# Hybrid encoder trunk: the last output projection computed as two Strassen products

## The chip, the cores and the metric

The kernel runs on one NeuronCore of a Trainium2 chip. The metric is the device time of one execution in microseconds; the figure for the kernel before is the median of three runs. The profile is of one separate execution.

## What is computed

Two encoder layers over 512 tokens with 2048 features, then an RMS norm, all in float32. Cut to what matters:

```python
def hybrid_layer(x, ...):
    proj = rms_norm(x, norm_w) @ w_in                  # 2048 -> 6144 columns
    o_attn = attention(q, k, v)                        # 1024 features
    o_conv = c_b * conv3(c_c * c_in)                   # 512
    o_sgu  = gelu(u) * (W_s norm(gelu(v)) + b)         # 512
    mixed  = concat(rms_norm(o_i, branch_w_i) * silu(gate_i))   # 2048
    return x + mixed @ w_out                           # 2048 -> 2048
y = rms_norm(layer2(layer1(x)), final_norm_w)
```

## The kernel before

Feature tiles (128 features on the partitions, 512 tokens along them) are kept as pairs: `split` writes a rounded part H on ACT (L96) and the rest L on DVE (L97). `product` takes one block of 512 output columns: `load_pair` (L76) fetches the weights of two feature tiles in one 512 KB transfer into a `wr` buffer, each tile is split into `wH` and `wL` (`split_weight`, L183 and L184, where a column scale is needed), and for each of the four output tiles three matmuls (L202) are added up: H·H, L·H, H·L. A product is 16 tiles x 4 x 3 = 192 matmuls. The pool `wp` gives `wr`, `wH` and `wL` three buffers each, so weights can be split at most a little ahead of the matmuls. The output projection reads the feature tiles `mH[0..15]`, `mL[0..15]`: tiles 0 to 7 are attention (`mA`), 8 to 11 convolution (`mc`), 12 to 15 the gating unit (`ms`).

The gating unit is last. After the last input projection (`win[l, 11]`) its rows go through Silu (L495), a multiply (L496), a block transpose on DVE (`tr.put`, L143), a 1 MB write to DRAM (`mv<-blk`, L149), four reads back (`rearr<-mv`, L153) and the split into `ms` tiles.

In layer 2 the output projection gives token-major rows. Blocks 0 to 2 of 512 columns are `product` calls; the residual x of each is rebuilt by `residual(b)`: an add of xH and xL (L527), a DVE transpose (L529), a write `mx<-p` (L531) and reads `xt<-mx` (L534). Row sums of squares are collected on ACT (L550), and the rows are multiplied by the final norm weight on GpSimd (L551). Block 3 is done last from weights that are all split ahead into `wfH`, `wfL` (in the freed `x{k}` buffers), one tile of 128 tokens after another, so that the end of each tile (L599 to L613) runs under the matmuls of the next.

The order of the instructions on each engine's queue is not that of the program: it is planned when the kernel is built (`TileContext(nc, schedule_with_timeline_sim=True)`), with an estimated duration for each instruction. Of the instructions whose inputs and buffers are free by that plan, the one that is earlier in the program goes first. On the chip each queue keeps that order. All large transfers are issued by SyncE (SP).

Of the kernel before, what the change touches and what calls it, by code (L numbers as in the profile page):

```python
# [8 lines left out]
F32 = mybir.dt.float32  # L9
# [5 lines left out]
P = 128  # L15
# [6 lines left out]
NQ = 8  # L22
NKV = 2
EPS = 1e-6
SCALE = HD ** -0.5


def f32(ap):
    return ap.bitcast(F32)
# [3 lines left out]
def trunk_kernel(ctx: ExitStack, tc: tile.TileContext, xT, win, wout, wcols, convw, qkw, sgun,  # L33
# [15 lines left out]
    def nm(s):  # L49
        uid[0] += 1  # L50
        return f"{s}_{uid[0]}"
# [134 lines left out]
    def product(src, cols, Hs, Ls, feature_major, before=None):  # L186
# [16 lines left out]
                                         stop=(k == KT - 1 and i == 2))  # L203
        return acc

    sqx = Squares()

    xraw = [big.tile([P, 4, S], F32, tag="mA", name=f"xraw{i}", bufs=4) for i in range(4)]
# [12 lines left out]
    def load_both(kp):  # L221
# [14 lines left out]
            first.append(broadcast_x(first[0]))  # L236
        return raw

    for l in range(L):
        banks.update(seq=["acc"] * 4, at=0)  # L240
        wc = lay.tile([P, 2, KT], F32, tag="wc", name=nm("wc"), bufs=2)
        nc.scalar.dma_start(out=wc, in_=wcols[l])
# [157 lines left out]

        mH, mL = [None] * KT, [None] * KT

        def finish(sq, inv, os, first, dst):
            R = broadcast_rows(token_rstd(sq.t, inv, "b"))
            for i, o in enumerate(os):
                nc.vector.scalar_tensor_tensor(out=o, in0=o, scalar=wc[:, 1, first + i:first + i + 1], in1=R,
                                               op0=ALU.mult, op1=ALU.mult)
                h_, l_ = dst(i)
                split(h_, l_, o)
                mH[first + i], mL[first + i] = h_, l_  # L410

        sqc = Squares()
# [33 lines left out]
        mA = [big.tile([P, ST, S], F32R, tag="mA", name=nm("mA"), bufs=4) for _ in range(4)]  # L446
        finish(sqa, 1.0 / 1024, oat, 0, lambda i: (mA[i // 4][:, i % 4], mA[2 + i // 4][:, i % 4]))

        finish(sqc, 1.0 / 512, oc, 8,
               lambda i: tuple(big.tile([P, S], F32R, tag="qb", name=nm("mc"), bufs=8) for _ in range(2)))  # L450

        acc = product(win[l, 9], nw, xH, xL, False)
        vnH = big.tile([P, ST, S], F32R, tag="kv", name=nm("vnH"), bufs=2)
# [45 lines left out]
        for st in range(ST):  # L499
            tr.put(st, gu[:, st])  # L500
        tr.move()
        for e in range(4):
            mH[12 + e], mL[12 + e] = [big.tile([P, S], F32R, tag="qa", name=nm("ms"), bufs=8) for _ in range(2)]
            split(by_block(mH[12 + e]), by_block(mL[12 + e]), tr.get(e))

        if l < L - 1:
            sqx = Squares()
            for b in range(4):
                acc = product(wout[l, b], bw, mH, mL, True)
                for e in range(4):  # L510
                    d = 4 * b + e
                    t = T()
                    nc.vector.tensor_tensor(out=t, in0=acc[e], in1=f32(xL[d]), op=ALU.add)
                    nc.vector.tensor_tensor(out=t, in0=t, in1=f32(xH[d]), op=ALU.add)
                    sqx.add(t)
                    split(xH[d], xL[d], t)

    fr = [lay.tile([P, S], F32, tag=tag, name=nm("fr")) for tag in ("sn", "swH", "swL", "Rx")]
    for b in range(4):
        nc.sync.dma_start(out=fr[b], in_=frow[b * S:(b + 1) * S].partition_broadcast(P))  # L520
    def residual(b):
        e_ = big.tile([P, 4, 4, P], F32, tag="o" if b == 0 else "kv", name=nm("xt"), bufs=1 if b == 0 else 2)
        m = dram.tile([P, 4, 4, P], F32, tag="mx", name=nm("mx"))
        for e in range(4):
            d = 4 * b + e
            t = T()
            nc.vector.tensor_tensor(out=t, in0=f32(xH[d]), in1=f32(xL[d]), op=ALU.add)  # L527
            blk = T("p")
            nc.vector.transpose(out=blk.rearrange("p (b s i) -> p s b i", b=4, i=32),  # L529
                                in_=t.rearrange("p (s b j) -> p s b j", b=4, j=32))  # L530
            nc.sync.dma_start(out=m[:, e], in_=blk.rearrange("p (b f) -> p b f", b=4))  # L531
        mv = m.rearrange("(a j) e b f -> b j e a f", a=4)
        for q in range(4):
            nc.sync.dma_start(out=e_[32 * q:32 * q + 32], in_=mv[q])  # L534
        return e_.rearrange("p e a (s i) -> p s (e a) i", i=32)
# [5 lines left out]
    xt = []  # L541
    for b in range(3):
        xt.append(residual(b))
        acc = product(wout[L - 1, b], bw, mH, mL, False)
        for st in range(ST):
            v = xt[b][:, st]
            nc.vector.tensor_tensor(out=v, in0=grouped(acc[st]), in1=v, op=ALU.add)
        for st in range(ST):
            v = xt[b][:, st]
            nc.scalar.activation(grouped(T()), v, AF.Square, accum_out=sums[st][:, b:b + 1])  # L550
            nc.gpsimd.tensor_tensor(out=v, in0=v, in1=grouped(fr[b]), op=ALU.mult)  # L551

    xq = [T("qr") for _ in range(ST)]
    m = dram.tile([P, 4, 4, P], F32, tag="mx", name=nm("mx"))
    for e in range(4):
        t = T()
        nc.vector.tensor_tensor(out=t, in0=f32(xH[12 + e]), in1=f32(xL[12 + e]), op=ALU.add)
        blk = T("p")
        nc.vector.transpose(out=blk.rearrange("p (b s i) -> p s b i", b=4, i=32),
                            in_=t.rearrange("p (s b j) -> p s b j", b=4, j=32))  # L560
        nc.sync.dma_start(out=m[:, e], in_=blk.rearrange("p (b f) -> p b f", b=4))
        nc.gpsimd.tensor_copy(out=xq[3][:, e * P:(e + 1) * P], in_=t[:, 3 * P:])
    mv = m.rearrange("(a j) e b (s i) -> b s j e a i", a=4, i=32)
    for st in range(3):
        for q in range(4):
            nc.sync.dma_start(out=xq[st][32 * q:32 * q + 32].rearrange("p (e a i) -> p e a i", e=4, a=4),
                              in_=mv[q, st])

    wf = []
    for kp in range(KT // 2):  # L570
        raw = load_pair(wout[L - 1, 3, kp])
        for j in range(2):
            k = 2 * kp + j
            H = res.tile([P, S], F32R, tag=f"x{k}", name=f"wfH{k}", bufs=2)
            Lo = res.tile([P, S], F32R, tag=f"x{k}", name=f"wfL{k}", bufs=2)
            split_weight(raw[:, j], bw(k), H, Lo)
            wf.append((H, Lo))
    part = sm.tile([P, ST], F32, tag="part", name="part", bufs=1)
    accs = accumulators()
    for st in range(ST):  # L580
        ss = slice(st * P, (st + 1) * P)
        p_ = part[:, st:st + 1]
        nc.vector.tensor_reduce(out=p_, in_=sums[st][:, :3], axis=AX.X, op=ALU.add)
        nc.vector.tensor_scalar(out=p_, in0=p_, scalar1=1.0 / D, scalar2=EPS, op0=ALU.mult, op1=ALU.add)
        acc = accs[st]
        if st == 3:
            for e in range(4):
                es = slice(e * P, (e + 1) * P)
                nc.tensor.matmul(acc[:, es], xq[3][:, es], ident, start=(e == 0), stop=False)
        for k in range(KT):  # L590
            H, Lo = wf[k]
            nc.tensor.matmul(acc, mH[k][:, ss], H, start=(st < 3 and k == 0), stop=False)  # L592
            nc.tensor.matmul(acc, mL[k][:, ss], H, start=False, stop=False)  # L593
            nc.tensor.matmul(acc, mH[k][:, ss], Lo, start=False, stop=(k == KT - 1))  # L594
        su = small(1)
        y = acc
        if st < 3:
            y = xq[st]
            nc.vector.tensor_tensor(out=y, in0=acc, in1=y, op=ALU.add)  # L599
        nc.scalar.activation(T(), y, AF.Square, accum_out=su)  # L600
        v = small(1)
        nc.vector.tensor_scalar(out=v, in0=su, scalar1=1.0 / D, scalar2=p_, op0=ALU.mult, op1=ALU.add)
        r = small(1)
        nc.gpsimd.tensor_tensor(out=r, in0=v, in1=negh[:, :1], op=ALU.pow)
        for b in (0, 2, 1, 3):
            o = T("p" if b % 2 else "t")
            if b == 3:
                nc.vector.scalar_tensor_tensor(out=o, in0=y, scalar=r, in1=fr[3], op0=ALU.mult, op1=ALU.mult)
            elif b == 2:
                nc.vector.tensor_scalar(out=grouped(o), in0=xt[b][:, st], scalar1=r, scalar2=None, op0=ALU.mult)  # L610
            else:
                nc.scalar.activation(grouped(o), xt[b][:, st], AF.Copy, scale=r)
            nc.sync.dma_start(out=out[ss, b * S:(b + 1) * S], in_=o)  # L613


def _columns():
# [51 lines left out]
```

## Time and profile before

| | |
|---|---|
| median of 3 runs | 1524.43 us (1522.11 to 1527.09) |
| span of the profiled execution | 1521.4 us, first to last instruction |
| TensorE busy | 1503.8 us (99%), 6630 matmuls |
| VectorE, ScalarE, GpSimd busy | 887.7, 625.5 and 74.5 us |
| DMA | 203.09 MB, mean 133 GB/s |

The page gives no other time of the profiled execution than its span; the span is 3.0 us under the median of the runs. The span runs from the first to the last instruction, and busy shares are means over stages with different limits.

### The profile page before, as it was taken

The page shows a single profiled execution, that of the slowest core. Times are in us where ns is not written, and L with a number is a line of the kernel's source. Part 1 is how long each engine was busy: PE and PEld are TensorE (multiplying, and loading weights), DVE is VectorE, ACT ScalarE, POOL GpSimd, SP SyncE. Part 2 cuts the span into 40 slices and gives each one's busy share as a digit, 9 for nine tenths or more (in the row PEclk, how much of TensorE's full clock was granted, in tenths as well). Part 3 has the DMA queues.
Part 4 walks back from the last instruction along what each step waited for, and adds up shares of the span by engine and source line. Part 5 has one row for each costly group of instructions (what it writes and reads, how often), then busy time and mean ns, then how long its engine had stood idle before and what let it go on. Part 6 is the DMA issues. An engine that isn't in the chain of part 4 may idle for free.

```text
span 1521.4 us, 18115 instructions
## 1 busy us (share of the span) xinstructions
PE 1503.8 (99%) x6630; PEld 1240.6 (82%) x6630; DVE 887.7 (58%) x1652; ACT 625.5 (41%) x1057; POOL 74.5 (5%) x72
## 2 busy tenths in 40 slices
PE   9999999999999999999999999999999999999997
PEld 7888878888888888888888887888888888878876
DVE  7667788745446534454446777896454573445562
ACT  7334365544334433333334344564343443332342
POOL 0111000000000100000000110000000010001120
PEclk9999999999999999999999999999999999999999
DMA  7345566733323334333334346676333333465544
GB/s 265 111 103 148 175 194 202 204 100 98 97 87 96 102 96 139 111 97 87 108 93 124 110 134 183 208 207 180 97 97 97 91 97 104 139 168 152 136 160 139
DMA packets 75402, 203.09 MB, mean 133 GB/s; under 512 B 14256, under 2 KB 21680, under 8 KB 72496
## 3 DMA queue, kind: packets, MB, share of 16 engines
q1 hardware_dynamic: 75024, 201.90, 45.4%
q8 instruction: 52, 0.85, 0.2%
q14 instruction: 38, 0.31, 0.1%
q10 hardware_dynamic: 288, 0.03, 0.0%
HBM read 169.39 MB, written 32.51 MB: 133 GB/s over the span
## 4 chain that ended last, share of the span: by engine, by line
PE 91%; DMA 4%; DVE 2%; issue 1%; ACT 1%; SPq 0%; ACTq 0%; POOLq 0%; DVEq 0%
PE acc L202 64%; PE sc L202 19%; DMA rearr<-mv 1%; DMA mv<-blk 1%; PE ps L371 1%; PE ps L372 1%; PE ps L370 1%; PE sc L344 1%; PE sc L345 1%; PE sc L346 1%; DMA wr<-in_wout 1%; PE sc L594 1%; DMA xt<-mx 0%; PE sc L592 0%; PE sc L593 0%
## 5 line engine op out<-in xcount | busy, mean ns | idle before, releaser
L184 DVE SCALAR_TENSOR_TENSOR wL<-wr,wc,wH 128x512 fp32r<-128x512 f32 x412 | 306.0, 747 | 395.8 <-ACT wH L183 376.9
L183 ACT ACTIVATE wH<-wr,wc 128x512 fp32r<-128x512 f32 x412 | 296.3, 723 | 532.2 <-PE acc L202 418.8
L202 PE MATMUL acc<-xL,wH 128*128 128x512 f32 x672 | 261.4, 389 | 0.0
L202 PE MATMUL acc<-xH,wH 128*128 128x512 f32 x672 | 260.8, 389 | 0.0
L202 PE MATMUL acc<-xH,wL 128*128 128x512 f32 x672 | 245.2, 389 | 0.0
L202 PE MATMUL acc<-wH,xH 128*128 128x512 f32 x608 | 237.2, 391 | 0.7 <-ACT wH L183 0.6
L202 PE MATMUL acc<-wH,xL 128*128 128x512 f32 x608 | 236.8, 390 | 0.0
L202 PE MATMUL acc<-wL,xH 128*128 128x512 f32 x608 | 213.5, 390 | 0.1
L202 PEld LDWEIGHTS acc<-xH,wH 128*128 128x128 f32 x672 | 126.2, 188 | 26.4
L202 PEld LDWEIGHTS acc<-xL,wH 128*128 128x128 f32 x672 | 126.1, 188 | 26.3
L202 PEld LDWEIGHTS acc<-xH,wL 128*128 128x128 f32 x672 | 126.1, 188 | 26.1
L202 PEld LDWEIGHTS acc<-wH,xH 128*128 128x128 f32 x608 | 114.2, 188 | 26.0 <-ACT wH L183 1.8
L202 PEld LDWEIGHTS acc<-wL,xH 128*128 128x128 f32 x608 | 113.9, 188 | 24.3 <-DVE wL L184 0.5
L202 PEld LDWEIGHTS acc<-wH,xL 128*128 128x128 f32 x608 | 114.3, 188 | 23.7
L97 DVE TENSOR_TENSOR wL<-wr,wH 128x512 fp32r<-128x512 f32 x84 | 57.4, 691 | 96.9 <-ACT wH L96 77.4
L96 ACT CAST wH<-wr 128x512 fp32r<-128x512 f32 x84 | 52.1, 623 | 134.3 <-PE acc L202 80.8
L353 ACT ACTIVATE p<-sc,sa 128x512 f32<-128x512 f32 x64 | 43.8, 685 | 62.2 <-DVE sa L350 58.0
L202 PE MATMUL sc<-wH,xL 128*128 128x512 f32 x160 | 62.3, 389 | 0.0
L202 PE MATMUL sc<-wH,xH 128*128 128x512 f32 x160 | 62.3, 389 | 0.0
L103 POOL TENSOR_TENSOR s<-s,negh 128x4 f32<-128x4 f32 (+2 forms) x40 | 43.3, 1082 | 371.4 <-DVE s L101 358.7
L202 PE MATMUL sc<-wL,xH 128*128 128x512 f32 x160 | 59.7, 390 | 0.0
L114 POOL TENSOR_TENSOR rc<-s,negh 128x4 f32<-128x4 f32 x6 | 7.6, 1273 | 881.3 <-DVE s L113 881.3
(259 smaller groups left out, 2214.5 us busy)
## 6 DMA issues: line engine op xcount, KB each, us to landing
wr<-in_win SPq DMA_DIRECT2D x191, 512.0 KB, 3.7
wr<-in_wout SPq DMA_DIRECT2D x64, 512.0 KB, 3.7
mv<-blk SPq DMA_DIRECT2D x22, 1024.0 KB, 4.7
rearr<-mv SPq DMA_DIRECT2D x88, 256.0 KB, 5.3
mx<-p SPq DMA_DIRECT2D x16, 256.0 KB, 3.1
xraw<-in_xT SPq DMA_DIRECT2D x7, 512.0 KB, 9.8
xt<-mx SPq DMA_DIRECT2D x12, 256.0 KB, 5.8
out_y<-t SPq DMA_DIRECT2D x8, 256.0 KB, 2.7
```

What stands on the lines that cost most here:

```text
L96: nc.scalar.copy(H, src)
L97: nc.vector.tensor_tensor(out=Lo, in0=src, in1=f32(H), op=ALU.subtract)
L103: nc.gpsimd.tensor_tensor(out=r, in0=v, in1=negh[:, :n], op=ALU.pow)
L183: nc.scalar.activation(wH, raw, AF.Copy, scale=c)
L184: nc.vector.scalar_tensor_tensor(out=wL, in0=raw, scalar=c, in1=f32(wH), op0=ALU.mult, op1=ALU.subtract)
L202: nc.tensor.matmul(acc[e], a, b, start=(k == 0 and i == 0), stop=(k == KT - 1 and i == 2))
L344: nc.tensor.matmul(sc, qH[:, ss], kH, start=True, stop=False)
L345: nc.tensor.matmul(sc, qH[:, ss], kL, start=False, stop=False)
L346: nc.tensor.matmul(sc, qL[:, ss], kH, start=False, stop=True)
L353: nc.scalar.activation(p, sc, AF.Exp, scale=SCALE, bias=nm_, accum_out=su)
L370: nc.tensor.matmul(po, a, pH[:, t], start=(t == 0), stop=False)
L371: nc.tensor.matmul(po, a, pL[:, t], start=False, stop=False)
```

## The change

The 2048 x 2048 output projection of layer 2 is taken as two products, each over two column blocks (0 and 1, then 2 and 3). In each, the contraction is cut into features 0 to 1023 and 1024 to 2047, the tokens into two halves of 256, and the columns into the two blocks. Seven half products (p = 1 to 7; each 8 feature tiles x 2 token tiles x 3 matmuls) stand for eight. What is needed for that:

- Sums and differences of the feature tiles (`differences`, four DVE operations on 128 x 256 for each k of 0 to 7), then split (`sums_of`) into the `x{k}` buffers. For k = 0 to 3 they are made after `finish`, before `win[l, 9]`; for k = 4 to 7 they need the gating unit's tiles, which are first scaled and copied on ACT (`raw`).
- Sums of weights, made by transfers: GpSimd issues transfers that add DRAM rows to a loaded buffer (`add_rows`, with `accum_op`). X[kp] is loaded for p = 1 and added to for p = 5, 6 and 4; p = 7 loads a `wr` buffer and adds to it.
- Three pairs of accumulator banks: p = 1, 6, 7, 4 use `c1`, p = 5, 3 use `c2`, p = 2 uses `c3`; the rows xt are added to or subtracted from after each.
- The residual's transposes and writes to DRAM move into layer 1's output projection, 16 of each; the adds xH + xL are gone. In layer 2 only the reads are left.
- At the end p = 4 of the second product is held: weights split ahead, 24 matmuls for each token tile. `leave(st)` takes the place of L596 to L613; the identity matmuls are gone.

```diff
+        if last:
+            for k in range(4):
+                v = nraw[k // 2][:, k % 2]
+                differences(v[:, 0], v[:, 1], v[:, 2], v[:, 3], oat[k], oc[k])
...
+        if last:
+            for k in range(4):
+                sums_of(k, v[:, 0:2], v[:, 2:4])
         for e in range(4):
-            split(by_block(mH[12 + e]), by_block(mL[12 + e]), tr.get(e))
+            nc.scalar.activation(by_block(raw), tr.get(e), AF.Copy, scale=wc[:, 1, 12 + e:13 + e])
+            split(mH[12 + e], mL[12 + e], raw)
+            differences(n12[:, 0], n12[:, 1], n34[:, 0], n34[:, 1], oat[4 + e], raw)
+            sums_of(4 + e, n12, n34)
...
+                    nc.vector.transpose(out=blk.rearrange("p (b s i) -> p s b i", b=4, i=32),
+                                        in_=t.rearrange("p (s b j) -> p s b j", b=4, j=32))
+                    nc.sync.dma_start(out=rowsd[b][:, e], in_=blk.rearrange("p (b f) -> p b f", b=4))
...
+    def add_rows(dst, src):
+        nc.gpsimd.dma_start(out=dst, in_=src, accum_op=ALU.add)
...
+        def weights(p, kp):
+            if p == 1:
+                nc.sync.dma_start(out=X[kp], in_=s0[kp])
+                return X[kp]
+            if p == 2:
+                return load_pair(s0[4 + kp])
+            if p == 3:
+                return load_pair(s1[4 + kp])
+            if p == 7:
+                y = load_pair(s1[4 + kp])
+                add_rows(y, s1[kp])
+                return y
+            add_rows(X[kp], {5: s1[kp], 6: s1[4 + kp], 4: s0[4 + kp]}[p])
+            return X[kp]
...
+        for p in order:
+            for kp in range(4):
+                w = weights(p, kp)
+                for j in range(2):
+                    split(H, Lo, w[:, j])
+                    for t in range(2):
+                        matmuls(bank[t], p, k, t, H, Lo)
...
+    pair(0, 1, (1, 2, 5, 6, 3, 7, 4), False)
+    residual(2)
+    residual(3)
+    pair(2, 3, (1, 5, 6, 3, 7, 2, 4), True)
```

## Rows read from the trace of the kernel before

**Rows 1.** The page: busy time of each engine, share, instructions.

```profile
PE 1503.8 (99%) x6630; PEld 1240.6 (82%) x6630; DVE 887.7 (58%) x1652; ACT 625.5 (41%) x1057; POOL 74.5 (5%) x72
```

**Rows 2.** The chain in order of time, layer 1: start us, us, what.

```profile
671.59 43.52 PE acc L202 x192
```

**Rows 3.** Timeline of PE: start us, us, engine, line, operation.

```profile
1334.73 0.61 PE L202 MATMUL sc<-wH,mA 128*128 128x512 f32 x2
...
1360.29 0.73 PE L202 MATMUL sc<-wH,mc 128*128 128x512 f32 x2 [0.92 <-ACT wH L96]
...
1513.10 0.39 PE L594 MATMUL acc<-wfL,ms 128*128 128x512 f32 x1
```

**Rows 4.** Windows: length; PE, PEld, DVE, ACT, POOL busy (count); clock; DMA share; GB/s.

```profile
1356.50:1367.40 10.90, 9.91 (x43) 7.57 (x42) 5.50 (x9) 5.20 (x9) 0.00 (x0) 1.00 0.62 168
...
1470.00:1482.00 12.00, 10.74 (x47) 8.41 (x46) 12.00 (x22) 5.57 (x12) 7.93 (x8) 1.00 0.28 95
```

**Rows 5.** Groups by line: count, busy us, mean ns, idle before.

```profile
L97 DVE TENSOR_TENSOR wL<-wr,wH 128x512 fp32r<-128x512 f32 x84 | 57.4, 691 | 96.9 <-ACT wH L96 77.4
...
L96 ACT CAST wH<-wr 128x512 fp32r<-128x512 f32 x84 | 52.1, 623 | 134.3 <-PE acc L202 80.8
...
L302 DVE TENSOR_TENSOR t<-t,cs 128x256 f32<-128x256 f32 x32 | 12.0, 416 | 0.1
...
L551 POOL TENSOR_TENSOR xt<-xt,fr 128x512 f32<-128x512 f32 x12 | 18.7, 1585 | 153.4 <-ACT t L550 153.4
...
L103 POOL TENSOR_TENSOR s<-s,negh 128x1 f32<-128x1 f32 x8 | 5.0, 626 | 85.2 <-DVE s L101 84.9
```

**Rows 6.** Groups by line, DVE, 1400 to 1440 us.

```profile
L527 DVE TENSOR_TENSOR t<-xH,xL 128x512 f32<-128x512 f32 x4 | 5.8, 1492 | 0.0
```

**Rows 7.** Timeline of SP and ACT, the gating unit's way in layer 2.

```profile
1340.48 0.33 SPq L149 DMA_DIRECT2D mv<-blk  x1
...
1340.86 3.69 SPq L534 DMA_DIRECT2D xt<-mx  x4
...
1346.12 2.71 SPq L153 DMA_DIRECT2D rearr<-mv  x4
...
1359.09 0.62 ACT L96 CAST ms<-rearr 128x512 fp32r<-128x512 f32 x1 [5.96 <-DMA rearr<-mv]
```

**Rows 8.** Timeline of SP and ACT, the same way in layer 1.

```profile
590.14 0.33 SPq L149 DMA_DIRECT2D mv<-blk  x1
...
603.43 1.14 ACT L96 CAST ms<-rearr 128x512 fp32r<-128x512 f32 x2 [4.85 <-DMA rearr<-mv]
```

**Rows 9.** Window after the last matmul, columns as in rows 4.

```profile
1518.00:1521.40 3.40, 0.00 (x0) 0.00 (x0) 0.00 (x0) 0.00 (x0) 0.00 (x0) 0.60 0.43 150
```

**Rows 10.** Timeline of PE, the first matmuls.

```profile
1.44 4.63 PE L89 MATMUL pw<-onesr 128*128 128x512 f32 x10 [1.44 <-DVE onesr L84]
```

**Rows 11.** The page: DMA issues, KB each, median us to landing.

```profile
wr<-in_wout SPq DMA_DIRECT2D x64, 512.0 KB, 3.7
...
mv<-blk SPq DMA_DIRECT2D x22, 1024.0 KB, 4.7
```

**Rows 12.** Tile view of rearr, 1340 to 1400 us.

```profile
DMA to landing us min/median/max: 9.3/10.3/10.8
```

**Rows 13.** Windows at the ends of layer 1's output blocks.

```profile
716.00:727.00 11.00, 11.00 (x51) 9.09 (x50) 10.62 (x18) 6.30 (x12) 0.00 (x0) 1.00 0.32 93
...
760.00:765.00 5.00, 4.93 (x22) 3.77 (x22) 4.84 (x9) 2.09 (x5) 0.00 (x0) 1.00 0.05 19
```

**Rows 14.** Timeline of the end: ACT and SP.

```profile
1513.57 0.60 ACT L600 ACTIVATE t<-acc 128x512 f32<-128x512 f32 x1 [8.10 <-issue]
...
1516.65 0.90 SPq L613 DMA_DIRECT2D out_y<-p  x2
```

**Rows 15.** Windows before and during that way.

```profile
1330.00:1340.00 10.00, 10.00 (x46) 8.29 (x45) 6.59 (x11) 5.48 (x8) 0.00 (x0) 1.00 0.30 95
...
1340.00:1360.00 20.00, 19.37 (x86) 15.71 (x84) 4.65 (x8) 4.02 (x7) 0.00 (x0) 1.00 0.99 236
```

More of the change, by code (lines that the diff above doesn't have):

```diff
@@ L24 @@
 EPS = 1e-6
+HALF = S // 2
 SCALE = HD ** -0.5
@@ L204, in product, with differences, sums_of @@
         return acc
+    NT = [None] * 8
+    def differences(n1, n2, n3, n4, lo, hi):
+        a, b = lo[:, :HALF], lo[:, HALF:]
+        c, d = hi[:, :HALF], hi[:, HALF:]
+        nc.vector.tensor_tensor(out=n1, in0=b, in1=d, op=ALU.subtract)
+        nc.vector.tensor_tensor(out=n2, in0=n1, in1=a, op=ALU.subtract)
+        nc.vector.tensor_tensor(out=n3, in0=a, in1=b, op=ALU.subtract)
+        nc.vector.tensor_tensor(out=n4, in0=n2, in1=c, op=ALU.add)
+    def sums_of(k, n12, n34):
+        got = []
+        for kk, n in ((k, n12), (k + 8, n34)):
+            H = res.tile([P, 2, HALF], F32R, tag=f"x{kk}", name=nm("nH"), bufs=2)
+            Lo = res.tile([P, 2, HALF], F32R, tag=f"x{kk}", name=nm("nL"), bufs=2)
+            split(H, Lo, n)
+            got += [(H[:, i], Lo[:, i]) for i in range(2)]
+        NT[k] = got
     sqx = Squares()
@@ L237, in load_both @@
         return raw
+    rowsd = []
     for l in range(L):
+        last = l == L - 1
         banks.update(seq=["acc"] * 4, at=0)
@@ L408, in finish @@
                 h_, l_ = dst(i)
-                split(h_, l_, o)
+                split(h_, l_, o[:, :n])
                 mH[first + i], mL[first + i] = h_, l_
@@ L508, in trunk_kernel @@
             for b in range(4):
+                rowsd.append(dram.tile([P, 4, 4, P], F32, tag="mx", name=nm("mx"), bufs=4))
                 acc = product(wout[l, b], bw, mH, mL, True)
@@ L520, in trunk_kernel @@
         nc.sync.dma_start(out=fr[b], in_=frow[b * S:(b + 1) * S].partition_broadcast(P))
[L521 to L535, printed above, removed]
@@ L537, in grouped @@
     def grouped(ap):
         return ap.rearrange("p (g i) -> p g i", i=32)
-    sums = [sm.tile([P, 4], F32, tag="sf", name=nm("sf"), bufs=ST) for _ in range(ST)]
[L541 to L594, printed above, removed]
-        su = small(1)
[L596 to L605, printed above, removed]
-            o = T("p" if b % 2 else "t")
[L607 to L610, printed above, removed]
-            else:
-                nc.scalar.activation(grouped(o), xt[b][:, st], AF.Copy, scale=r)
-            nc.sync.dma_start(out=out[ss, b * S:(b + 1) * S], in_=o)
@@ new lines, in trunk_kernel, with residual @@
+    xt = {}
+    def residual(b):
+        mv = rowsd[b].rearrange("(a j) e b f -> b j e a f", a=4)
+        if b < 3:
+            e_ = big.tile([P, 4, 4, P], F32, tag="o" if b == 0 else "kv", name=nm("xt"), bufs=1 if b == 0 else 2)
+            for q in range(4):
+                nc.sync.dma_start(out=e_[32 * q:32 * q + 32], in_=mv[q])
+            v = e_.rearrange("p e a (s i) -> p s (e a) i", i=32)
+            for st in range(ST):
+                xt[b, st] = v[:, st]
+        else:
+            mv = rowsd[b].rearrange("(a j) e b (s i) -> b s j e a i", a=4, i=32)
+            for st in range(ST):
+                r = T("qr")
+                for q in range(4):
+                    nc.sync.dma_start(out=r[32 * q:32 * q + 32].rearrange("p (e a i) -> p e a i", e=4, a=4),
+                                      in_=mv[q, st])
+                xt[b, st] = grouped(r)
@@ new lines, in add_to, with take_from, squares, weighted @@
+    def add_to(bank, b, st):
+        nc.vector.tensor_tensor(out=xt[b, st], in0=grouped(bank), in1=xt[b, st], op=ALU.add)
+    def take_from(bank, b, st):
+        nc.vector.tensor_tensor(out=xt[b, st], in0=xt[b, st], in1=grouped(bank), op=ALU.subtract)
+    def squares(b, st):
+        nc.scalar.activation(grouped(T()), xt[b, st], AF.Square, accum_out=sums[st][:, b:b + 1])
+    def weighted(b, st):
+        nc.gpsimd.tensor_tensor(out=xt[b, st], in0=xt[b, st], in1=grouped(fr[b]), op=ALU.mult)
@@ new lines, in leave @@
+    def leave(st):
+        su = small(1)
+        nc.vector.tensor_reduce(out=su, in_=sums[st], axis=AX.X, op=ALU.add)
+        r = rstd(su, 1, 1.0 / D)
+        for b in (2, 0, 1, 3):
+            o = T("p" if b % 2 else "t")
+            if st < 2 or b == 2:
+                nc.vector.scalar_tensor_tensor(out=grouped(o), in0=xt[b, st], scalar=r, in1=grouped(fr[b]),
+                                               op0=ALU.mult, op1=ALU.mult)
+            elif b == 1:
+                nc.vector.tensor_scalar(out=grouped(o), in0=xt[b, st], scalar1=r, scalar2=None, op0=ALU.mult)
+            else:
+                nc.scalar.activation(grouped(o), xt[b, st], AF.Copy, scale=r)
+            nc.sync.dma_start(out=out[st * P:(st + 1) * P, b * S:(b + 1) * S], in_=o)
@@ L616, in _columns @@
+    residual(0)
+    residual(1)
+    pair(0, 1, (1, 2, 5, 6, 3, 7, 4), False)
+    residual(2)
+    residual(3)
+    pair(2, 3, (1, 5, 6, 3, 7, 2, 4), True)
 def _columns():
```

84 lines of the change are left out of this document (81 added, 3 removed).

## Prediction

> **What bounds the kernel now.** I read the page first: TensorE is busy for 99% of the span [rows 1], so time moves only where matmuls are taken away or where TensorE is made to wait. The chain in order of time shows one whole product in layer 1 as 192 matmuls in 43.52 us [rows 2]: 0.2267 us each, 10.88 us for 48. Then the timeline of layer 2's output projection: its first matmul starts at 1334.73, its last at 1513.10 [rows 3], so it takes 178.6 us. Its 768 matmuls are worth 174.1 us of that; 4.5 us are waits and the 16 identity matmuls. The windows show where: 1.0 us idle around 1360, where the gating unit's tiles arrive, and 1.3 us around 1475 [rows 4]. The reader is to see that almost everything else in this stage is hidden under matmuls, so that cover, not work, is what the change spends.
>
> **What is removed.** One half product in eight: 14 x 10.88 = 152.3 us of matmuls in place of 178.6 with its waits, a saving of 26.3 us if nothing new waited. Also gone are the adds xH + xL and four small GpSimd copies, and six of twelve GpSimd multiplies; all these lie under matmuls now, and I give nothing for them. One of them did harm to VectorE: beside the GpSimd multiply of 1585 ns [rows 5] the adds took 1492 ns [rows 6] where the like operation takes 691 [rows 5]. Fewer of these multiplies is a small help; I count nothing.
>
> **The gating unit's way loses its cover.** In the kernel before, tiles 12 to 15 are wanted after 12 of a product's 16 tiles, 32.6 us after 1334.73. In the new order p = 1 needs none of them and p = 2 only its second half, so they are wanted after 10.88 + 5.44 = 16.3 us, at 1351.05. They arrive later: the write goes out at 1340.48, four reads `xt<-mx` are issued behind it, the reads back at 1346.12, and ACT's first split runs at 1359.09, after 5.96 us of waiting for them [rows 7]. The new chain adds a scaled copy before the split (0.6 us by the split's row), then split and subtraction, 0.62 and 0.69 [rows 5]: first matmul at 1361.0, a wait of 10.0 us. Behind the arrival VectorE has four bursts, one for each tile: a subtraction, four differences at 0.42 (the 128 x 256 row [rows 5]) and two more subtractions, 3.7 us against 1.36 us of matmuls. Taken strictly tile by tile, the fourth tile comes 7 us after TensorE wants it; with the needed subtractions first, not at all. I take 3. What could fill this wait is p = 5 on its first four tiles (5.4 us), but `wH` has three buffers, and the splits for p = 2's second half are ready and earlier in the program: they take all three and hold them until the gating unit arrives. So I take 13.0 us. Below, the way could be as quick as in layer 1, 590.14 to 603.43 [rows 8], 13.3 us after the write: 4.7 us of wait. Above, 10 + 7 + 6 (a rival below) = 23.
>
> A pause this long has no row in TensorE's stream. What precedes a fall of the granted clock is seen at the end: it is 0.60 on average over the last 3.4 us, which begin 4.5 us after the last matmul [rows 9]. And ten matmuls at the start take 4.63 us [rows 10] for 2.27 at full clock (2.4 GHz), as at 1.2 GHz. I add 2.4 us once for coming back; nothing to 2.4 for the shorter waits below.
>
> **The accumulating transfers.** There are 32, issued by GpSimd, and no row shows one. Their landing time L is the unknown. Below: a plain load of the same 512 KB, 3.7 us. Above: 10.3 us, the median of the reads back in the crowded stretch [rows 11, 12]. I take the 1024 KB write, 4.7 [rows 11], since the destination is read and written too, plus the smallest GpSimd instruction, 0.63 [rows 5], for the issue: 5.3. For p = 5, 6 and 4 that is hidden: X[kp] is free when the previous user has split it, and wanted 10.88 us later less 1.4 for the splitting, so L up to 9.4 costs nothing. SyncE is not delayed, since these are on GpSimd's queue; there the pow and multiplies of ends of products queue with them, but X is free some 10 us earlier than these are ready, so the plan puts the transfers first.
>
> p = 7 is the exception: it loads a `wr` buffer, then adds to it, right behind p = 3, which uses the same three buffers. Counted from p = 3's first matmul, its second pair is split by 2.8, so p = 7's first load is issued then and lands at 6.8; the sum is there at 6.8 + L, split by 8.8 + L. Only then can the fourth load of p = 7 start (the buffers go round), land at 12.8 + L, be summed at 12.8 + 2L, and its first tile be ready at 14.1 + 2L. TensorE wants it at 10.88 + 3 x 2.72 = 19.0. The wait is 2L - 4.9: at 5.3, 5.7 us, and 11.4 for both products; 5.0 at L = 3.7, 31.4 at 10.3.
>
> **What stays hidden.** A split pair of weights now serves 6 matmuls, 1.36 us, in place of 12: ACT needs 0.62 and VectorE 0.69 for it [rows 5], and the two adds from PSUM bring VectorE to 6.9 of 10.88 us in a half product, so it keeps up; with that cover gone each add would cost its 0.69. For k = 0 to 3 the 16 differences and 8 splits are 12 us of VectorE and 5 of ACT, under three input projections of 43.5 us with VectorE 58% busy on average [rows 1]; I cost them at nothing, 12 us if they were in the way. SyncE's reads of the residual stay (12 of 256 KB, and 16 small ones for 12), and the first four come at the same point as now, when the gating unit's rows have left their buffer.
>
> **Small ones.** p = 4 directly follows p = 7 in the same banks in the first product, so its first matmul waits for one subtraction from PSUM: 0.7 us (0 to 1.4). In layer 1, 16 transposes of 0.69 [rows 5] and 16 writes come to the ends of the blocks. There VectorE is busy 10.62 of 11 us already and TensorE lost 0.07 us once [rows 13]; cover runs out after two tiles of matmuls, 5.4 us. SyncE has only weight loads there. I take 1.5 us over four ends; 0 if the slack holds, 8 if most of each 2.8 us shows. In the end, ACT took the last square straight from PSUM at 1513.57 and the last output was issued at 1516.65 [rows 14]; `leave` needs an add (0.69) and a reduction first: 0.9 us (0.7 to 1.5).
>
> **Sum.** -26.3 + 13.0 + 2.4 + 11.4 + 0.7 + 1.5 + 0.9 = +3.6 us: span 1525.0. The profiled execution's span is 3.0 us under the median of the runs, so 1528 us. 0.3% is 4.6 us, about what a measurement can tell from no change: 1519.8 to 1529.0 counts as the same.
>
> **Rivals.** (a) *The waits are half as long.* The plan lets the first half of p = 5 in (13.0 becomes 7.6) and the transfers land like plain loads (5.0 for p = 7), and layer 1 costs nothing: -26.3 + 7.6 + 2.4 + 5.0 + 0.7 + 0.9 = -9.7, 1514.7 us. For it: DMA is at 0.30 of its engines just before [rows 15], and the plan did move the residual's work forward of the gating unit's, so it does reorder. Against it: three `wH` buffers.
>
> (b) *Accumulating transfers are slow.* At L = 10.3, p = 7 waits 31.4 and each p = 6 another 0.9: 21.8 us more, 1549.8 us, slower. Each microsecond of L is worth 4 in the sum, so from L = 5.6 this alone carries the forecast over 1529. For it: the destination must be read; against it: 9.3 to 10.8 us [rows 12] was seen only where the engines were full.
>
> (c) *They collide with the gating unit's reads.* Between 1340 and 1360 the DMA engines are at 0.99 [rows 15]; before, 3.0 us of them moved 950 KB, so 1.65 for 512 KB. p = 5's four transfers, at twice that, are 13.2 us, half of them after 1340: the tiles come 6.6 us later, 1534.6 us. The Trainium skill, "DMA: Bandwidth & Descriptors", section "Issuing engines are not separate DMA queues", says that transfers issued by any engine run on the same 16 DMA engines and interleave; by that rule this case decides. No run here has a GpSimd transfer yet to show it; the 0.99 agrees that there is no room.
>
> (d) *Layer 1's ends* cost 8 us in place of 1.5: 1534.5 us.
>
> The Trainium skill, "DMA: Bandwidth & Descriptors", section "Anatomy of one DMA — SWDGE (gpsimd) path", gives about 2.0 us plus bytes over 436 GB/s for such a transfer: an estimate of 3.2 us for 512 KB. By it p = 7 would wait 1.5 us each time and the sum would be 8.4 us lower. The plain load here takes 3.7 [rows 11], so the Trainium skill's figure is short even for that.
>
> **Chances.** (a) 0.35, forecast 0.33, (b) 0.14, (c) 0.14, (d) 0.04. The forecast's own range is 1519 to 1537. Faster by over 0.3%: 0.29 of (a) and 0.02 of the forecast, 0.31. Same: 0.06 of (a), 0.18 of the forecast, 0.02 of (c), 0.01 of (d), 0.27. Slower: the rest, 0.42. The range 1507 to 1548 leaves out some 0.04 of (a) below and 0.08 of (b) above.
>
> **What would show it.** Right: TensorE idle for some 10 us between the first and second half of p = 2, released by ACT's or VectorE's work on `ms`; idle of 5 to 6 us inside each p = 7, released by a GpSimd transfer; none inside p = 5, 6, 4. Wrong: matmuls of p = 5 between those of p = 2; an accumulating transfer that lands in under 4 or over 7 us; the granted clock at 1.00 through the wait; idle at 716 to 770 us of over 2 us. The prediction fails most easily through L, which counts four times.

## The result and the profile after

The changed kernel took 1563.08 us (median of 4 runs, 1561.01 to 1568.56), beside 1523.32 for the kernel before on the same chip: ratio 1.0263, interval 1.024 to 1.0287. It is slower by 40 us, and above the top of the range, 1548. The profiled execution has a span of 1561.8, 40.4 more than before.

The page, busy time of each engine (against [rows 1]), and the DMA issues with KB each and median us to landing (against [rows 11]):

```profile
PE 1495.0 (96%) x6526; PEld 1227.7 (79%) x6526; DVE 931.4 (60%) x1745; ACT 657.6 (42%) x1121; POOL 91.0 (6%) x94
...
wr<-in_wout SPq DMA_DIRECT2D x56, 512.0 KB, 3.6
wx<-in_wout POOLq DMA_DIRECT2D x24, 512.0 KB, 7.7
...
wr<-in_wout POOLq DMA_DIRECT2D x8, 512.0 KB, 7.4
```

TensorE is busy for 9 us less only, though 21.8 us of matmuls are gone (174.1 less 152.3), and the accumulating transfers (`POOLq`) land in 7.4 to 7.7 us, twice a plain load. The waits of TensorE, us in total, times, longest:

```profile
PE acc L663 <- ACT wH L97: 23.4, 6, 6.0
PE sc L663 <- ACT ms L97: 19.0, 2, 18.2
...
PE acc L203 <- DVE t L558: 2.0, 1, 2.0
```

TensorE's timeline with the pauses, as [rows 3]: the gating unit's tiles, and product 7 twice, first pair.

```profile
1372.22 1.22 PE L663 MATMUL sc<-wH,ms 128*128 128x512 f32 x2 [18.22 <-ACT ms L97]
...
1421.38 0.79 PE L663 MATMUL acc<-wH,nH 128*128 128x512 f32 x1 [6.04 <-ACT wH L97]
...
1435.15 0.50 PE L663 MATMUL acc<-wH,nH 128*128 128x512 f32 x1 [2.58 <-ACT wH L97]
```

SP's timeline, as [rows 7]:

```profile
1337.36 6.60 SPq L589 DMA_DIRECT2D qr<-mx  x9
1344.06 0.65 SPq L150 DMA_DIRECT2D mv<-blk  x1
1344.76 4.39 SPq L580 DMA_DIRECT2D xt<-mx  x4
1349.19 9.01 SPq L589 DMA_DIRECT2D qr<-mx  x2
1358.30 1.19 SPq L77 DMA_DIRECT2D wr<-in_wout  x1
1359.53 0.56 SPq L589 DMA_DIRECT2D qr<-mx  x1
1360.14 2.95 SPq L154 DMA_DIRECT2D rearr<-mv  x4
```

The read-back goes out 16.1 us after the write (5.6 before): small reads of the residual's block 3 have come ahead of it, and two of them hold SP for 9 us. Windows, columns as in [rows 4]:

```profile
1354.00:1372.20 18.20, 0.00 (x1) 0.00 (x0) 2.63 (x5) 1.99 (x4) 0.00 (x0) 0.64 1.15 208
1372.20:1377.20 5.00, 4.88 (x12) 3.21 (x12) 5.00 (x12) 3.87 (x7) 0.00 (x0) 0.62 1.15 249
1421.40:1427.30 5.90, 5.90 (x14) 4.64 (x15) 4.09 (x7) 3.45 (x8) 0.00 (x0) 0.51 1.00 234
1427.30:1432.60 5.30, 5.27 (x23) 3.98 (x22) 1.05 (x2) 0.62 (x1) 0.88 (x1) 1.00 0.61 142
```

The DMA share (the time that packets took, as a share of the 16 engines; it can pass 1) is above 1 through the wait, and after each of the five longest pauses (18.22, 6.04, 5.83, 5.25 and 3.47 us) TensorE works at 1.2 GHz: 14 matmuls in 5.9 us behind product 7's first pause, 23 in 5.3 once the granted clock is at 1.00. The five stretches of this stage in which TensorE works at a granted clock of 0.50, behind the gating unit's tiles, product 7, product 6 of the second pair, and product 7 twice:

```profile
1372.22:1376.00 3.78, 3.78 (x8) 2.65 (x9) 3.78 (x10) 2.74 (x5) 0.00 (x0) 0.50 1.19 199
1421.38:1427.20 5.82, 5.82 (x14) 4.56 (x15) 4.01 (x7) 3.47 (x8) 0.00 (x0) 0.50 1.01 232
1482.01:1485.20 3.19, 3.19 (x8) 2.51 (x9) 3.19 (x6) 2.65 (x5) 0.89 (x1) 0.50 0.20 17
1505.91:1509.10 3.19, 3.19 (x8) 2.52 (x9) 2.02 (x4) 2.84 (x7) 0.00 (x0) 0.50 0.96 154
1521.11:1526.20 5.09, 5.09 (x12) 4.03 (x13) 2.57 (x4) 2.02 (x4) 0.00 (x0) 0.50 0.39 109
```

They are 21.1 us long; at half speed they cost half of that, 10.5 us: 1.9 behind the gating unit's pause, 2.9, 1.6 and 2.5 behind product 7's, 1.6 behind product 6's.

**The ledger.** The output projection runs from 1336.60 to 1548.11, 211.5 us against 178.6: 152.3 of matmuls, 44.2 of pauses and 15.0 left over. Of the 15.0, 10.5 are slow clock by these windows; the other 4.5 are stalls too short to be listed as pauses, and what they wait for is not shown. The pauses are the gating unit's tiles 19.5 (18.22 and two short ones), product 7 19.7 (6.04 + 2.58 + 5.83 + 5.25), product 6 of the second pair 3.5, the rest 1.5. With a start 1.9 later and 5.6 more behind the last matmul (13.7 for 8.1): 32.9 + 1.9 + 5.6 = 40.4. The 5.6 fit the order: TensorE ran product 2 of the second pair among the matmuls of product 4, so three of the four token tiles became ready between 1540.1 and 1542.8, the fourth at the end (with another order, in e8 below, 9.3 are left behind the last matmul). GpSimd's four `pow`, which open the four departures:

```profile
1544.55 0.56 POOL L104 TENSOR_TENSOR s<-s,negh 128x1 f32<-128x1 f32 x1 [12.61 <-DVE s L102]
1548.28 0.55 POOL L104 TENSOR_TENSOR s<-s,negh 128x1 f32<-128x1 f32 x1 [3.17 <-DVE s L102]
1551.97 0.54 POOL L104 TENSOR_TENSOR s<-s,negh 128x1 f32<-128x1 f32 x1 [3.15 <-DVE s L102]
1554.41 0.54 POOL L104 TENSOR_TENSOR s<-s,negh 128x1 f32<-128x1 f32 x1 [1.89 <-DVE s L102]
```

### The profile page after: what moved, and what is told of

Read it like the earlier page. It is cut to its first block, busy times and chain, and to the rows that moved or that the text cites. A ratio compares the mean times of both kernels' runs of the same rounds, so it can differ in the third digit from the quotient of the medians.

```text
span 1561.8 us, 18214 instructions
## 1 busy us (share of the span) xinstructions
PE 1495.0 (96%) x6526; PEld 1227.7 (79%) x6526; DVE 931.4 (60%) x1745; ACT 657.6 (42%) x1121; POOL 91.0 (6%) x94
## 4 chain that ended last, share of the span: by engine, by line
PE 81%; DMA 6%; issue 6%; DVE 4%; ACT 2%; POOL 1%; SPq 0%; ACTq 0%; POOLq 0%; DVEq 0%
PE acc L203 56%; PE sc L203 16%; DMA wr<-in_wout 2%; DMA mv<-blk 1%; PE acc L663 1%; DMA wx<-in_wout 1%; PE acc L664 1%; PE acc L665 1%; DMA rearr<-mv 1%; PE ps L394 1%; PE ps L392 1%; PE ps L393 1%; POOL wx L635 1%; PE sc L366 1%; PE sc L367 1%
## 5 line engine op out<-in xcount | busy, mean ns | idle before, releaser
L185 DVE SCALAR_TENSOR_TENSOR wL<-wr,wc,wH 128x512 fp32r<-128x512 f32 x400 | 297.6, 748 | 373.6 <-ACT wH L184 351.8
L184 ACT ACTIVATE wH<-wr,wc 128x512 fp32r<-128x512 f32 x400 | 287.5, 723 | 506.6 <-PE acc L203 406.2
L98 DVE TENSOR_TENSOR wL<-wr,wH 128x512 fp32r<-128x512 f32 x96 | 66.8, 711 | 96.7 <-ACT wH L97 78.4
L97 ACT CAST wH<-wr 128x512 fp32r<-128x512 f32 x96 | 58.5, 621 | 141.2 <-DMA wr<-in_wout 48.7
L663 PE MATMUL acc<-wH,nH 128*128 128x512 f32 x128 | 54.7, 428 | 23.4 <-ACT wH L97 23.4
```

Of the source, the lines that this page charges most:

```text
L184: nc.scalar.activation(wH, raw, AF.Copy, scale=c)
L185: nc.vector.scalar_tensor_tensor(out=wL, in0=raw, scalar=c, in1=f32(wH), op0=ALU.mult, op1=ALU.subtract)
L663: nc.tensor.matmul(bank, a, H, start=begin, stop=False, skip_group_check=True)
```

## The experiments

The runs are numbered e1 to e14. The theory: accumulating transfers land late, so product 7's ring costs 2L - 4.9 each time, and they fill the DMA engines through which the gating unit's rows travel. The rival: SP's order of issue delays those rows, whatever the sums do.

**No sums, and none for product 7.**

```
 def add_rows(dst, src):
-    nc.gpsimd.dma_start(out=dst, in_=src, accum_op=ALU.add)
+    return                                   # e1
...
-            add_rows(y, s1[kp])              # e3, product 7 alone
```

Expected of e1:

> The changed kernel without any of the 32 accumulating transfers (the weight sums are left out, so p = 5, 6, 4 and 7 use unsummed weights). Theory (slow landing meets three wr buffers): the waits inside p = 6 and p = 7, 23 us, vanish with the slow matmuls behind them, some 8 us: about 1532 us. The wait for the gating unit's tiles stays at 15 us or more of 18.2, because SyncE's queue still holds the small residual reads ahead of the write and the reads back. Rival (the sums crowd the DMA engines and so delay the gating unit's rows): that wait falls to 10 us or less too, about 1522 us.

Expected of e3:

> The changed kernel without the 8 accumulating transfers of p = 7 (its weights are left unsummed); the other 24 stay. Theory (load, then sum, in a ring of three wr buffers): the four waits in p = 7, 19.7 us, vanish with the slow matmuls behind them, some 7 us: about 1536 us, and the 3.5 us wait in p = 6 of the second product stays. Rival (the DMA engines as a whole are too full): only the share of 8 in 32 of the waits goes, about 1555 us.

Without any sum 1523.86 us, ratio 0.9992 (0.9981 to 1.0003): the sums cost 39 us, all that the change had lost. The gating unit's wait is 8.2, not 18.2, so the rival was right on it:

```profile
1366.16 1.22 PE L663 MATMUL sc<-wH,ms 128*128 128x512 f32 x2 [8.18 <-ACT ms L97]
...
1340.55:1512.06 171.51, 159.15 (x673) 128.82 (x671) 114.41 (x181) 86.34 (x158) 10.20 (x8) 0.95 0.46 118
```

But the saving of 26 us does not appear here either, with no sum in the way and a DMA share of 0.46. The second line is the window of e1's output projection: 171.5 us for 178.6. Pauses take 12.0 of it (8.18, 3.20 and 0.65), the slow clock behind them 5.3, and 5.5 more than before lie behind the last matmul, nearly as in the changed kernel.

Without product 7's sums 1535.41 us, ratio 1.0065 (1.005 to 1.008): product 7's pauses are gone, as the theory expected, the gating unit's wait (18.08) is not. The two costs are separate, and the pauses of 19.7 were worth 27.7. The 8.0 on top are mostly slow clock: the stretches behind product 7's pauses cost 7.0 by the windows above.

**Plain transfers from GpSimd** (`accum_op` dropped).

Expected of e4:

> The 32 GpSimd transfers as plain copies of the same bytes (the sums are left out: each overwrites its buffer). Theory (adding to the buffer is what is slow): they land in 4 to 5 us instead of 7.4 to 7.7, p = 7 waits 2L - 4.9, so 3 to 5 us in each product instead of 8.6 and 11.1, under 5 us of pause the clock holds: about 1543 us. Rival (issue by GpSimd is what is slow): they still land in about 7 us and the time stays at 1558 us or more.

1548.24 us, ratio 1.0149 (1.0121 to 1.0177). The landings, and GpSimd's DMA queue (packets, MB, share of the 16 engines' span), first in the changed kernel, then here:

```profile
wx<-in_wout POOLq DMA_DIRECT2D x24, 512.0 KB, 4.7
...
wr<-in_wout POOLq DMA_DIRECT2D x8, 512.0 KB, 5.0
...
q0 software_dynamic: 4608, 16.78, 5.8%
...
q0 software_dynamic: 4608, 16.78, 3.4%
```

So it is the adding that takes L from 4.7 to 7.7, more than the issue by GpSimd. It also holds the engines longer for the same bytes: 5.8% of 1561.8 us is 2.8 us of all 16 engines for each transfer, 3.4% of 1551.5 us is 1.6. Product 7 still pauses 6.0 and 8.0 us, where 2L - 4.9 gives 5.1 at L = 5.0. The gating unit still waits 16.5: for that, the bytes are enough.

**Who delays the gating unit's rows.** e2: reads of block 3 held until product 2's result is added; e6: sums held until the rows have arrived; e7: the reads of blocks 0, 1 and 3 held until the first of the four tiles is split.

```
+    nc.vector.tensor_copy(r[:, :1], xt[0, 1][:, 0, 0:1])           # e2
...
+arrived = nc.gpsimd.tensor_copy(mark, tr.get(3)[:, 0, 0, 0:1])     # e6
...
+with tc.issue_after(arrived.ins):                                  #     around add_rows
...
+    nc.vector.tensor_copy(r[:, :1], f32(mH[12])[:, :1])            # e7, and into xt
```

Expected of e2:

> The changed kernel with the 16 small residual reads of block 3 held back until p = 2 is done (a one-column copy that depends on it is written into each buffer first). Theory (SyncE's queue order): the reads back are issued as soon as the write has landed, some 8 to 10 us earlier, and the wait of 18.2 us falls to 8 to 10: about 1554 us; the waits in p = 7 stay. Rival (the sums crowd the DMA engines): the rows still arrive late, the wait stays at 15 us or more, 1560 us or more.

Expected of e6:

> GpSimd reads one column of the gating unit's arrived rows and issues every accumulating transfer behind that; nothing else is changed. Theory (product 5's four sums and the residual's reads fill the DMA engines while the gating unit's rows travel): the wait for those rows falls from 18.2 us to 8 to 12 (it was 8.2 without sums), and product 5, whose first sum now starts when the rows are there and lands 8 to 9 us later behind 5.4 us of product 2's second half, waits 2 to 6: 1563 - 4 = 1559, 1553 to 1564. Rival (SP's own order of issue is what is late): the wait stays at 15 or more and product 5's wait comes on top: 1566 or more.

Expected of e7:

> The residual's reads (first two blocks and the small ones of block 3) are held until the first tile of the gating unit's rows is split; the sums are not held. Theory of the order on SP (9 small reads stand ahead of the gating unit's write, 4 + 2 reads between its write and its read-back): the write is issued some 6 us earlier, the read-back 10 to 16 us earlier, the wait falls from 18.2 to 4 to 9: 1563 - 12 = 1551, 1546 to 1556. Theory of the sums' transfers in the DMA engines: SP is free earlier, but the read-back still waits for a write that shares the engines with four accumulating transfers: wait 11 to 15 us, 1557 to 1562. Held reads may also meet the sums of product 6, as in the run that held the small ones only (1573).

| kernel | write to read-back issued | landing, median | first wait for `ms` | time, ratio |
|---|---|---|---|---|
| changed | 16.1 | 7.2 | 18.2 | 1563.08, 1.0263 |
| block 3's reads held | 11.2 | 9.9 | 15.8 | 1573.01, 1.0304 (1.0279 to 1.0329) |
| sums held | 7.0 | 6.9 | 8.2 | 1567.44, 1.0278 (1.0263 to 1.0293) |
| reads of blocks 0, 1, 3 held | 7.6 | 8.5 | 10.0 | 1568.77, 1.029 (1.0273 to 1.0307) |
| both held (e8, with other edits) | 3.9 | 5.6 | 3.0 | 1531.94, 1.0043 (1.0026 to 1.006) |

e2 went as its rival said (15.8), and was slower still. Holding the sums or the reads of blocks 0, 1 and 3 brings the read-back some 9 us nearer to the write, so neither theory has the wait alone: SP stands in its issues where reads with short rows and GpSimd's transfers go out together. The same two small reads took SP 9.01 us in the changed kernel and 6.93 with plain transfers (e4), 2.69 without any (e1), 2.48 with the sums held (e6). A full DMA share alone does not tell them apart: it is 1.08, 1.13, 1.03 and 1.02 in these stretches. But no hold shortens the kernel. What was held meets what comes next; with the sums held, they go out beside block 3's last reads:

```profile
1365.18 21.32 SPq L589 DMA_DIRECT2D qr<-mx  x5
```

and product 6 of the first pair pauses 5.78, product 7 4.26 and 4.36. In e6 the wait fell as the theory said, the time did not: I had priced only product 5's wait. In e7 I had named the meeting with product 6's sums and given it no price.

**Product 7's sum into product 3's kept tiles, and all edits together.** e5 alone, then with both holds, the first pair's order in the second pair too (two token tiles leave during products 7 and 4), GpSimd's multiplies later.

```
-                y = load_pair(s1[4 + kp])
-                add_rows(y, s1[kp])
+                add_rows(kept[kp], s1[kp])                         # e5; kp = 3 in two T("p")
...
-    pair(2, 3, (1, 5, 6, 3, 7, 2, 4), True)
+    pair(2, 3, (1, 2, 5, 6, 3, 7, 4), True)                        # e8
```

Expected of e5:

> Product 7 adds s1[kp] to the four weight tiles that product 3 has loaded and keeps (three of the ring, one in two tiles that stand idle in this stage), in place of loading s1[4+kp] a second time and adding to that; nothing else is changed. Theory (a sum in the ring of three begins only when the tile is loaded, and the tile is loaded only when an earlier one is consumed, so each lap costs twice the landing less the work between): now every sum has all of product 3's 10.9 us ahead of it, against a landing of 7.5, so the 19.7 us of waits in product 7 go, with the slow clock behind them, as in the run without these sums: 1563 - 27 = 1536, 1532 to 1541. Rival (it is the accumulating itself that holds product 7 up, wherever it is added): waits of 4 us or more stay in each product 7, and the time stays above 1548.

Expected of e8:

> All three of the above, and: in the second pair the order of the products is that of the first (1, 2, 5, 6, 3, 7, 4), so that two of the four token tiles leave during products 7 and 4; GpSimd's multiplications of the first pair stand behind the second pair's sums of product 6. Sum if the terms are right and independent: first matmul at 1336.6, 152.3 of matmuls, 6 for the gating unit's rows, 3 for product 5, 0.7, 5 of slow clock, 9 of tail, 1.7 outside the span: 1514, 1506 to 1524; so faster than before by up to 1%. If the waits only move (a rival for all of these edits together: the same bytes have to pass at some time): above 1535.

e5: 1539.15 us, ratio 1.0095 (1.008 to 1.0111), no pause in product 7, as the theory expected. That speaks for the ring, not adding as such: with 10.9 us ahead of them the same sums cost at most the 3.7 us that part e5 from e3, which has none of them. (e5 also drops eight loads of 512 KB; the two effects are not separated.) e8: 1531.94 us, not 1514. One pause of 9.48 was new. VectorE's timeline shows its cause, an addition in its queue that waited for block 0's held rows, with the weights' splits behind it:

```profile
1381.07 1.29 DVE L614 TENSOR_TENSOR xt<-acc,xt 128x512 f32<-128x512 f32 x2 [8.09 <-DMA xt<-mx]
```

**Where the residual's reads go.** e9: block 0 free, block 2 behind product 3, block 3 behind product 4. e10: the same, and block 3's transposes out of layer 1's end. e11: e8 with the latter, and block 0 right behind the read-back on SP. e12: e11, and product 6's sum by GpSimd in SBUF, with product 3 ahead of product 6. e13: e11, and blocks 2 and 3 at product 3's and 6's place. e14: e13 with the residual's tiles read in long rows.

```
+    after_ = {1: lambda: f32(mH[12])[:, :1], 2: lambda: xt[1, 1][:, 0, 0:1], 3: lambda: xt[0, 2][:, 0, 0:1]}  # e9
...
+        nc.vector.tensor_tensor(out=t, in0=f32(xH[12 + e]), in1=f32(xL[12 + e]), op=ALU.add)   # e10, in layer 2
+        rows_of(3, e, t)
...
+    with tc.issue_after(tr.back.ins):                              # e11, block 0
...
+    nc.gpsimd.tensor_tensor(out=X[kp][:, j], in0=X[kp][:, j], in1=more, op=ALU.add)            # e12
...
+    if not final and p == 6: residual(3)                           # e13
...
+    nc.sync.dma_start(out=e_, in_=rowsd[b])                        # e14
```

Expected of e9:

> The combined kernel, with the residual's reads spread: block 0 is not held (it goes out while the gating unit's write lands), block 1 is held until the gating unit's first tile is split, block 2 until product 3's result is added, block 3 until product 4's result is added; the additions of products 1 and 2 in the first pair stand in program order behind product 5's third weight pair. Theory (in the combined run VectorE stood 8.09 us behind an addition that waited for block 0's held rows, and TensorE 9.48 behind it, with some 4 us of slow clock after): both go, the gating unit's read-back comes 2 us later for block 0's four reads ahead of it: 1531.9 - 9.5 - 4 + 2 = 1520, 1516 to 1525. Rival (the DMA engines are full from 1357 to 1437 whatever the order, so the wait goes to the next transfer): one gap of 5 us or more stays between 1360 and 1400, and the time at 1527 or more.

Expected of e10:

> The same, and block 3's four transposes are taken out of the end of layer 1 and made in layer 2 behind the last head, where VectorE is busy half of the time. Theory (VectorE, full at the end of layer 1, releases the next product's bank 2.0 us late because of these): the pause of TensorE at about 765 goes, 2 us less than the run beside it, 1518. Rival (VectorE is full there without them): the pause stays above 1 us and the two runs agree within 1 us.

Expected of e11:

> The combined kernel with the four transposes of block 3 out of the end of layer 1, and one thing else: the reads of the residual's block 0 stand right behind the gating unit's read-back on SP, not behind its arrival (blocks 1 to 3 stay held as in the combined kernel). Theory (in the combined kernel the 9.48 us pause came from block 0 alone, whose rows an addition on VectorE waited for): that pause and the slow clock behind it go, the gating unit's wait grows by 1 to 2 us for the transfers that run beside its rows, 2 us come from layer 1: 1531.9 - 9.5 - 4 + 2 - 2 = 1518, 1514 to 1524. Rival (the DMA engines are full there and the wait only changes its place, as in the run with the reads spread): 1529 to 1537, with a gap of 5 us or more at another transfer.

Expected of e12:

> The same, and product 6's sum is no transfer: product 3 runs ahead of product 6, its weights are kept, and GpSimd adds them to the running sum in SBUF (16 additions of 128x512 a pair in two). 4 MB less go through the DMA engines, and 8 of the 32 accumulating transfers are gone. If the DMA engines are what the stage waits for: 4 to 10 us less than the run beside it, where that one still waits for transfers, and nothing less where it does not. If GpSimd's additions (about 1.6 us each against 1.36 us of matmuls for the same weights) set the pace of product 6: up to 5 us more than the run beside it, in gaps of about 0.3 us per weight tile in both pairs.

Expected of e13:

> The kernel of the run with block 0's reads behind the read-back, and the residual's reads of blocks 2 and 3 held until product 6's (block 3) and product 3's (block 2) place in the first pair, by a copy from the tile that product 3's addition leaves. Theory (SP stood 15 and 20 us in the small reads of block 3 there, product 3's third weight pair waited behind them, and so did product 7's sum: 3.82 us and a slower clock): 1530.6 - 3.8 - 2 = 1525, 1521 to 1528. Rival (DMA engines are full, the wait moves): 1529 to 1535.

Expected of e14:

> The same, but the residual's tiles are read with their 8 KB or 2 KB rows as they lie in DRAM, one transfer for four: the same bytes in far fewer and longer packets, the residual's values in the wrong places. If the small rows of the residual (128 and 512 bytes) are what fills the DMA engines beside the sums: the sums land sooner (5 to 6 us for 7.3), the waits between 1355 and 1410 fall below 4 us together, 8 to 12 us less than the run beside it: 1514 to 1518. If the accumulating transfers fill them by themselves: within 3 us of the run beside it.

e9: 1539.27, ratio 1.01 (1.0084 to 1.0117): the rival was right, the wait moved. The pause of 9.48 went, one of 6.77 stands before the gating unit's tiles, and block 3's reads held SP for 18 us ahead of product 2's weights in the second pair, a pause of 5.87 there:

```profile
1435.18 18.27 SPq L593 DMA_DIRECT2D qr<-mx  x16
1453.56 6.36 SPq L77 DMA_DIRECT2D wr<-in_wout  x4
```

e10: 1538.08, ratio 1.0084 (1.0069 to 1.0098). Layer 1's pause is gone (4.93 of 5 us busy at 760, as in [rows 13]; 3.26 in the changed kernel), but a pause of 7.99 came up at 1385 that e9 does not have, so the two times do not measure it. e11: 1530.57, ratio 1.0042 (1.0028 to 1.0056), in the rival's range of time, but with no pause above 3.81. e12: 1539.43, ratio 1.0096 (1.0075 to 1.0118), slower by 8.9 than e11, more than the 5 that I had allowed: GpSimd's additions stand in the order of its queue and wait for product 3's weights (7.09 us once); less traffic did not pay for that. e13: 1524.91, ratio 1.0001 (0.9992 to 1.001), as its theory expected, and as long as the kernel before. e14: 1521.91, ratio 0.9977 (0.9966 to 0.9988), 3.0 us less than e13. Its waits between 1355 and 1410 are 5.5 us (9.7 in e13), yet its sums land no sooner (7.1 us for 6.6). What the long rows do change is SP's issue: block 1's reads take it 13.51 us in e13, the same bytes as one transfer 0.33 in e14, at a DMA share of 1.07 and 1.05 over the 13.5 us from there:

```profile
1359.88 13.51 SPq L596 DMA_DIRECT2D xt<-mx  x4
...
1358.91 0.33 SPq L595 DMA_DIRECT2D xt<-mx  x1
```

The windows 1337 to 1517 of the kernel before, e13 and e14:

```profile
1337.00:1517.00 180.00, 174.24 (x767) 142.52 (x765) 86.37 (x130) 56.75 (x105) 22.87 (x20) 1.00 0.55 152
```

```profile
1337.00:1517.00 180.00, 163.66 (x676) 129.15 (x674) 117.06 (x198) 88.68 (x164) 40.88 (x44) 0.95 0.87 192
```

```profile
1337.00:1517.00 180.00, 160.97 (x673) 125.73 (x671) 117.48 (x200) 88.91 (x165) 41.43 (x45) 0.97 0.79 195
```

The share of the DMA engines in this stage went from 0.55 to 0.87. Long rows take 0.08 of that away; without sums (e1) it is 0.46, so the sums and the weights they bring are the most of it. In e13 TensorE's stage is 1337.67 to 1514.84: 152.3 of matmuls, 14.1 of pauses, 10.8 left over, of which 6.6 are slow clock (13.1 us of work at 0.50). That is where the 26 us went, even with all these edits.

## Why the prediction was wrong

- **What held.** The matmuls saved: where nothing is late, TensorE runs them without a pause (20.0 us busy of 20 between 1457 and 1477, clock 1.00, beside a DMA share of 1.04; the line is below). No matmul of product 5 filled the gating unit's wait. The formula 2L - 4.9: at the measured 7.4 it gives 9.9 for each product 7; measured 8.6 and 11.1. The pauses stand before its first pair (6.04 and 5.83) and its fourth (2.58 and 5.25), where I had worked out one before the fourth; the sum is the same. The bank handed from product 7 to 4, 0.65 for 0.7. Layer 1, 1.97 for 1.5, in one place only.

```profile
1457.00:1477.00 20.00, 20.00 (x90) 16.55 (x89) 11.78 (x18) 7.89 (x13) 6.12 (x7) 1.00 1.04 193
```

- **L**, the term with the largest weight, was taken as 5.3 and measured 7.4 to 7.7: 19.7 us of pauses in place of 11.4. A landing of over 7 us was among my signs of being wrong. I had taken the row of a write of 1024 KB. A plain transfer from GpSimd lands in 4.7 to 5.0, and adding takes 2.4 to 3.0 more. The Trainium skill, "DMA: Bandwidth & Descriptors", section "Anatomy of one DMA — SWDGE (gpsimd) path", gives a fixed time plus bytes over a rate, by which 3.2 us is an estimate for this size. The runs show it short for both, the plain transfer and the accumulating one.
- **The gating unit's way**, 19.5 in place of 13.0. This is the step that failed in kind: I let the sums pass beside the gating unit's rows at no cost, with rival (c) at 0.14, and wrote that SyncE "is not delayed". It was, inside its own issues: the write went out 3.6 us later than before, the read-back 16.1 after the write for 5.6, and the rows then landed sooner, in 7.2 for 10.3. Rival (c) has the size, 6.6 for the 6.5 that were missing, by another path: it charged the engines' time to the rows' landing. That the sizes agree is luck. The section "Issuing engines are not separate DMA queues" of the same page of the Trainium skill says that all issuers share the engines, and the trace agrees as far as it goes: the share is 1.15 in the wait, and holding the sums takes 10 us off it. It does not tell that SP itself stands.
- **The slow clock**, 10.5 in place of 2.4 "once". I gave the short waits nothing to 2.4 in words and zero in the sum. Behind product 7's 6.04 us pause it cost 2.9, behind the 18.22 us one 1.9, and it fell behind 3.47 us too. For e4 I wrote that it holds under 5 us of pause; no run shows that, and in e4 it fell behind pauses of 4.33 and 4.58 (granted clock 0.50 in the 5.4 and 5.7 us after them).
- **Short stalls**, 4.5, for which the sum had no term.
- **The tail**, 5.6 in place of 0.9, and **product 6 of the second pair**, 3.5 in place of 0. For the latter I wrote that the plan puts the transfers ahead of GpSimd's multiplies. It did not: two multiplies, 3.20 us together, stood ahead of product 5's second sum at 1451. But the pause itself ended on ACT, by its timeline: the splits of product 4's weights (`vH`, split ahead) stood in its queue before those of product 6's sixth tile, and waited 4.79 us for a sum that product 6 did not need.

```profile
1480.30 1.14 ACT L97 CAST vH<-wx 128x512 fp32r<-128x512 f32 x2 [4.79 <-DMA wx<-in_wout]
1481.34 1.13 ACT L97 CAST wH<-wx 128x512 fp32r<-128x512 f32 x2
```

In all: gating 6.5, product 7 8.3, clock 8.1, short stalls 4.5, tail 4.7, product 6 3.5, and 1.3 of small ones make up the 36.8 between +3.6 and +40.4, but for rounding. Not settled: what the short stalls wait for, why short rows beside GpSimd's transfers hold SP, and what in the accumulating transfer takes its 2.4 to 3.0 us; 1.2 us more of the engines go to each.

## What to carry to other kernels

A change that trades matmuls for transfers spends the cover of the transfers that are already there. The share of the DMA engines in the stage does not price that by itself: here it went from 0.55 to nearly full, but TensorE ran 20 us without a pause at 1.04, and without any sum (0.46) the stage still gave back only 7 us. What cost time were single transfers that landed late: rows behind short-row reads in SP's queue, and sums in a ring of three buffers. e13's edits together were worth 38 us, 24 of them by e5's edit alone, and no version gave the saved 26 us back. So look for the transfer in a short ring and give its landing a whole product of cover, look at what stands ahead of an urgent transfer in the queue that issues it, and price a pause of TensorE together with the clock behind it: 1.6 to 2.9 us here behind pauses of 3.47 to 18.22.

## What was not expected of the hardware

- An accumulating transfer of 512 KB into SBUF lands in 7.4 to 7.7 us (median), a plain one from the same queue in 4.7 to 5.0, one from SP in 3.6 to 4.5.
- SP stands in the issue itself where reads with short rows go out beside GpSimd's transfers: two reads of 64 KB took 9.01 us, against 2.69 without sums, at a DMA share of 1.08 and 1.03; five took 21.32 in e6. One transfer with long rows took 0.33 where four with short rows and the same bytes took 13.51 (e14 and e13).
- An accumulating transfer took 2.8 us of the 16 engines for 512 KB, a plain one from the same queue 1.6.
- After a pause of 6.04 us TensorE ran at half speed for 5.8 us (granted clock 0.50); after one of 18.22, for 3.8.
